# The gate stage of a decoder trunk: squares written three tiles behind their tanh, and tanh results in four tiles of their own

## The chip, the core and the metric

The kernel runs on one core of a Trainium2 chip, as one launch. The metric is the device time of that launch in microseconds. Three executions of the kernel before took 2317.64, 2319.58 and 2322.39 us; the median, 2319.58 us, is the time that the change is measured against. The core has engines that run side by side and wait for each other by semaphores: PE (TensorE, the matmuls), DVE (VectorE), ACT (ScalarE), POOL (GpSimd) and SP (SyncE, which here only issues DMAs). Each engine works its own list of instructions strictly in the order in which it was built.

## The reference

Two layers work on an activation x of 512 tokens by 1024 features, all in float32. Per layer:

```
h  = RMSNorm(x)
A, B = attention(h), time mixing(h)        (two token mixers)
x += RMSNorm((sigmoid(gA)*A + sigmoid(gB)*B) @ W_out)
x += RMSNorm(W_down(gelu(a)*b)),  [a,b] = conv3(RMSNorm(x) @ W_up)
x += RMSNorm(sigmoid(x @ W_pg) * (p[i] @ W_ple))      <- the gate stage
```

The last line is the stage that the change touches. RMSNorm divides by the root of the mean square over the 1024 features of a token, so its factor for a token is known only once all eight feature tiles have been squared and summed.

## The kernel before, in words

x lies transposed: eight tiles (KT = 8) of 128 features by 512 tokens. The tokens are worked in two halves of 256 (`HALVES`, line 29), so that one half's norm can run beside the other half's matmuls. Weights and activations are split into a high and a low part, and each product is three matmuls, high by high, high weight by low activation, low weight by high activation (`mm3`, lines 250 to 252). In the trace the split parts have the names wh and wl or kwh and kwl (weights), xh and xl (x as the gate stage reads it), hh and hl (the next layer's input). A high part is written by ACT, a low part by DVE.

**The gate stage** is `pg`, a call of the generator `lin` (lines 945 to 979) that is resumed by `next(pg)` once for each half (line 1049). Per half it makes eight output tiles. The first three are interleaved over the eight feature tiles of x (`deep` = 3), so that they can start as soon as the first tile of x is final; the other five follow one after another. Each tile has 24 matmuls of 128x256. The results go to PSUM: tiles 0 to 2 of both halves and tiles 3 to 7 of the first half use the buffers pm, pm and pf (`PM`, line 102); tiles 3 to 7 of the second half use the pool of three buffers `PS`, under the name half (line 111).

When a tile is complete, `done` (line 950) does four things for it: ACT takes the tanh out of PSUM into a tile tg (line 1029), which frees the PSUM buffer; DVE makes yo = (tg + 1) * yo (line 1030); ACT squares yo into sq (`addsq`, line 293; the first tile's square goes straight to acc); and DVE adds sq to acc. tg and sq come from one pool S of four buffers. When all eight have been added, `rstd` (lines 279 to 291) makes the norm factor: PE sums acc over the partitions (ssq, line 284), DVE makes nv, a seed nry and three Newton steps (each nrt, nrt, nry), and PE spreads the factor over the partitions (rstd, line 290). `post_norm` (line 334) then makes, per feature tile, yo = yo * g * rstd and x = x + yo, on DVE.

The same `rstd` and `post_norm` stand ahead of the gate stage, for the result of W_down. There they hand over each x tile to `scaled`, which writes xh and xl for the gate matmuls. The second half of that norm runs beside the gate stage's first half.

**After the gate stage** of layer 0 come `seam` and `lead` (lines 1077 and 217): post_norm of each half, with hh and hl, and the first matmuls of the next layer (lead, and pm<-hh). After that of layer 1 comes the end of the kernel: post_norm of the first half, then of the second, and the DMAs of x.

**What sets the order.** The lists of the engines are made at build time by a scheduler with priorities. The order in which the Python code emits instructions is an instruction's priority; `turn` (line 1062) raises it for the norms, and for the second half holds the norm back behind a named matmul (`pin`). So the place at which `done` emits an instruction decides where it comes to stand in an engine's list, and also what the scheduler puts ahead of it.

Of the kernel before, what the change touches and what calls it, by code (L numbers as in the profile page):

```python
# [55 lines left out]
class Trunk:  # L56
# [287 lines left out]
    @staticmethod  # L344
    def row(t, k):
        return t[k * P:(k + 1) * P, :]
# [491 lines left out]
    def run(self):  # L838
        nc, tc, a = self.nc, self.tc, self.a
# [9 lines left out]
        G = self.alloc(xpool, "N", 30)  # L849
        A, S = self.alloc(xpool, "A", 4), self.alloc(xpool, "S", 5)  # L850
# [11 lines left out]
        for l in range(self.L):  # L862
# [68 lines left out]
            for m in range(KT):  # L931
                ps = self.proj(a["w_or"][l, m], yact)
# [9 lines left out]
            fp = xstack.enter_context(tc.tile_pool(name=f"ff{l}", bufs=1))  # L942
            G, X, Y, A, S = (self.alloc(fp, n, b) for n, b in (("G", 44), ("X", 8), ("Y", 8), ("A", 3), ("S", 4)))

            def lin(src, act, ys, ws, evac, n, deep=1, extra=None):

                acc = A("acc")
                self.res = ys, acc

                def done(m, ps, hs):  # L950
                    self.addsq(acc, evac(ys[m][:, hs], ps[:, hs], m, hs), hs, m == 0, S)
                for m in range(n):
                    if deep == 2 and m == 1:
                        raws = [self.raw_w(src(i), P, G) for i in range(n, KT)]
                    if deep == 2 and m == 2:
                        ws = [self.split_raw(r, G) for r in raws]
                    done(m, self.proj(src(m), act), slice(0, T))
                    if extra and 0 < m <= 4:
                        extra(m - 1)
                yield  # L960
                ws = [self.load_wk(src(n), S)] if ws is None else ws
                for hs in HALVES:
                    one = hs is HALVES[0]
                    pss = [self.PM("x") if i < 3 else self.PS("half") for i in range(deep)]
                    for k in range(len(act)):
                        for i in range(deep):
                            x_ = self.mm3(pss[i][:, hs], ws[i][k], tuple(x[:, hs] for x in act[k]), k == 0, k == len(act) - 1)
                        if k == 5:
                            self.pin = x_
                    for i in range(len(ws)):  # L970
                        if i < deep:
                            ps = pss[i]
                        else:
                            ps = self.PM("x") if i < 3 or one else self.PS("half")
                            self.proj_half(ps, ws[i], act, hs)
                        done(n + i, ps, hs)
                    if one:
                        yield
                yield
# [4 lines left out]
            ed = self.dt(f"ed{l}")  # L984
            ys = [Y("yo") for _ in range(KT)]
            wo = lin(lambda m: a["w_out"][l, m], mixed, ys, None, copy, 4, 2)
            next(wo)
            xs = []
# [18 lines left out]
            for m in range(KT):  # L1007
# [3 lines left out]
                ps = self.PM("f") if m % 2 else self.PT("ple")  # L1011
                for k, w in enumerate(self.whole(a["w_ple"][l, m], P, self.cls)):
# [6 lines left out]
            ys = [Y("yo") for _ in range(KT)]  # L1019
            gw = []  # L1020
            dn = lin(lambda m: a["w_dn"][l, m], u, ys, None, copy, KT - 1,
                     extra=lambda m: gw.append(self.keep_w(a["w_pg"][l, m], P, H)))
            next(dn)
# [1 line left out]
            fin = self.res  # L1025

            def ple(y, ps, m, hs):
                tg = S("tg")
                self.act(tg[:, hs], ps, AF.Tanh, scale=0.5)
                self.stt(y, tg[:, hs], 1.0, y, ALU.add, ALU.mult)  # L1030
                return y
            xa = [(G("xh", F32R), G("xl", F32R)) for _ in range(KT)]
            ys = []
            graw = [self.raw_w(a["w_pg"][l, m], P, G) for m in range(6, KT)]
            pg = lin(lambda m: a["w_pg"][l, m], xa, ys, gw, ple, 0, 3)
            next(pg)
            for hs in HALVES:
                with self.turn(hs):
                    self.post_norm(*fin, vv("fpost"), NORM_EPS, xs, hs, lambda k: self.scaled(xs[k], None, xa[k], hs))
                if hs is HALVES[0]:  # L1040
                    next(dn)
                    if hs is HALVES[0]:
                        with self.behind():
                            gw += [self.whole(a["w_pg"][l, m], P, "mf"[m - 4]) for m in range(4, 6)]
                            gw += [self.split_raw(r, G) for r in graw]
                            ys += [G("yo") for _ in range(KT)]
                            for m in range(KT):
                                self.dma(ys[m], row(ed, m))
                next(pg)
            ys, acc = self.res  # L1050
# [151 lines left out]
```

## Time and profile before

| | |
|---|---|
| median of three executions | 2319.58 us |
| profiled execution | 2329.03 us |
| its span, first to last instruction | 2327.3 us |
| mean granted TensorE clock over the span | 0.981 |
| PE busy | 2228.8 us, 96% of the span |
| DVE, ACT, POOL busy | 66%, 48%, 1% |
| gate stage of layer 0, matmuls | about 1116 to 1172 us |
| gate stage of layer 1, matmuls | about 2263 to 2308 us |

A row of the timeline reads: start, duration, engine, line, operation, output<-inputs, shape, count, and in brackets how long the engine had been idle and what ended that. Matmuls are pipelined, so that two of 0.28 us may start 0.12 us apart. "PEclk" in a table of windows is the TensorE clock that was granted, 1.00 being full speed. Lines are those of the kernel before; 125, 128 and 134 are the helpers `act`, `tt` and `stt`, so that a group there is known by its tile.

### The profile page before, as it was taken

What the parts mean: (1) busy time and instruction counts of PE and PEld (TensorE: products, weight loads), DVE (VectorE), ACT (ScalarE), POOL (GpSimd) and SP (SyncE); (2) the same over time, 40 slices, a digit from 0 to 9 for tenths busy, and PEclk for the clock granted to TensorE, in tenths of its full rate; (3) what the DMA queues carried; (4) which work ended last, traced back from release to release, by engine and by line L of the source; (5) the groups of instructions that cost most, each with busy time, mean ns of one, the idle gap of its engine ahead of it and who ended that gap; (6) DMA issues with size and microseconds to landing.
All of it is one profiled execution on the core that took longest, in us unless ns stands there. A gap on an engine that the chain in (4) does not pass through costs nothing. (4 is left out here: it accounts for less than half of the span.)

```text
span 2327.3 us, 39473 instructions
## 1 busy us (share of the span) xinstructions
PE 2228.8 (96%) x14340; PEld 1740.2 (75%) x14340; DVE 1546.9 (66%) x3683; ACT 1109.6 (48%) x2450; POOL 27.1 (1%) x86
## 2 busy tenths in 40 slices
PE   7999999999999999999899999998999999999997
PEld 6766776667689777788896677766777887777886
DVE  6764678767566777743877647778656667776346
ACT  5566455544444544432445655545443544444332
POOL 1000000000000000000000000000000000000000
PEclk9999999889999999999999999999999999999998
DMA  4532332245571423233234333333356623223432
GB/s 150 168 94 97 99 94 79 75 121 171 176 259 31 128 91 98 89 118 116 86 124 148 98 104 98 83 92 103 113 159 212 213 78 92 95 95 90 126 98 69
DMA packets 204515, 269.40 MB, mean 116 GB/s; under 512 B 71840, under 2 KB 84640, under 8 KB 204320
## 3 DMA queue, kind: packets, MB, share of 16 engines
q1 hardware_dynamic: 204320, 266.88, 37.3%
q8 instruction: 113, 1.85, 0.3%
q14 instruction: 82, 0.67, 0.1%
HBM read 218.95 MB, written 42.47 MB: 112 GB/s over the span
## 5 line engine op out<-in xcount | busy, mean ns | idle before, releaser
L155 DVE TENSOR_TENSOR wl<-w,wh 128x512 fp32r<-128x512 f32 (+2 forms) x574 | 373.9, 662 | 317.4 <-ACT wh L125 292.7
L125 ACT ACTIVATE wh<-w 128x512 fp32r<-128x512 f32 (+1 forms) x590 | 348.8, 604 | 477.8 <-PE pm L251 134.7
L250 PE MATMUL pm<-hh,wh 128*128 128x512 f32 x1040 | 423.0, 412 | 4.6 <-ACT wh L125 2.4
L252 PE MATMUL pm<-hh,wl 128*128 128x512 f32 x1040 | 417.1, 408 | 7.4 <-DVE wl L155 7.2
L251 PE MATMUL pm<-hl,wh 128*128 128x512 f32 x1040 | 416.3, 404 | 0.0
L250 PEld LDWEIGHTS pm<-hh,wh 128*128 128x128 f32 x1040 | 196.8, 189 | 63.3 <-ACT wh L125 11.2
L252 PEld LDWEIGHTS pm<-hh,wl 128*128 128x128 f32 x1040 | 196.9, 189 | 57.5 <-DVE wl L155 13.6
L251 PEld LDWEIGHTS pm<-hl,wh 128*128 128x128 f32 x1040 | 197.4, 190 | 44.1 <-issue 7.2
L250 PE MATMUL pf<-hh,wh 128*128 128x512 f32 x512 | 208.3, 407 | 9.5 <-ACT hh L125 3.6
L251 PE MATMUL pf<-hl,wh 128*128 128x512 f32 x512 | 203.7, 398 | 0.0
L252 PE MATMUL pf<-hh,wl 128*128 128x512 f32 x512 | 203.5, 398 | 0.1
L134 DVE SCALAR_TENSOR_TENSOR cv<-un,vec,cv 128x511 f32<-128x511 f32 (+1 forms) x176 | 130.5, 749 | 40.6 <-ACT cv L125 38.1
L250 PEld LDWEIGHTS pf<-hh,wh 128*128 128x128 f32 x512 | 96.2, 188 | 42.7 <-ACT wh L125 8.5
L252 PEld LDWEIGHTS pf<-hh,wl 128*128 128x128 f32 x512 | 96.6, 189 | 27.0 <-issue 4.4
L251 PEld LDWEIGHTS pf<-hl,wh 128*128 128x128 f32 x512 | 96.7, 189 | 19.6 <-issue 1.8
L125 ACT ACTIVATE cv<-un,vec 128x512 f32<-128x512 f32 x88 | 71.1, 814 | 66.7 <-DVE un L128 66.7
L250 PE MATMUL pm<-uh,wh 128*128 128x512 f32 (+1 forms) x248 | 89.2, 360 | 3.5 <-ACT wh L125 3.4
L252 PE MATMUL pm<-uh,wl 128*128 128x512 f32 (+1 forms) x248 | 89.3, 360 | 0.0
L251 PE MATMUL pm<-ul,wh 128*128 128x512 f32 (+1 forms) x248 | 88.9, 359 | 0.0
L128 DVE TENSOR_TENSOR acc<-acc,sq 128x256 f32<-128x256 f32 (+1 forms) x114 | 50.0, 463 | 31.2 <-ACT sq L125 30.5
L533 DVE CUSTOM_DVE_ANT_0 sm<-scores,tmask 128x256 f32<-128x256 f32 (+1 forms) x128 | 43.5, 385 | 37.3 <-PE scores L117 37.1
L697 DVE TENSOR_TENSOR Z<-rin,Z 128x126 f32<-128x126 f32 (+22 forms) x248 | 62.3, 251 | 4.3
(409 smaller groups left out, 4468.9 us busy)
## 6 DMA issues: line engine op xcount, KB each, us to landing
w<-in_w_up_dram SPq DMA_DIRECT2D x156, 256.0 KB
w<-in_w_dn_dram SPq DMA_DIRECT2D x80, 256.0 KB
w<-in_w_q_dram SPq DMA_DIRECT2D x32, 256.0 KB
w<-in_w_ga_dram SPq DMA_DIRECT2D x32, 256.0 KB
w<-in_w_k_dram SPq DMA_DIRECT2D x32, 256.0 KB
w<-in_w_r_dram SPq DMA_DIRECT2D x32, 256.0 KB
w<-in_w_v_dram SPq DMA_DIRECT2D x32, 256.0 KB
w<-in_w_gb_dram SPq DMA_DIRECT2D x32, 256.0 KB
```

The source lines that it names most:

```text
L125: return self.nc.scalar.activation(out=out, in_=in_, func=func, **kw)
L128: return self.nc.vector.tensor_tensor(out=out, in0=in0, in1=in1, op=op)
L134: return self.nc.vector.scalar_tensor_tensor(out=out, in0=in0, scalar=s, in1=in1, op0=op0, op1=op1)
L155: self.nc.vector.tensor_tensor(out=wl, in0=w, in1=wh.bitcast(F32), op=ALU.subtract)
L250: mm(ps, wh, ah, start=start, stop=False)
L251: mm(ps, wh, al, start=False, stop=False)
L252: return mm(ps, wl, ah, start=False, stop=stop).ins
L533: nc.vector.tensor_tensor_reduce(out=sm[i][:, par * 256:par * 256 + KW], in0=scs[par][:, x * 256:x * 256 + KW], in1=tm, scale=1.0, scalar= ...
L697: nc.vector.tensor_tensor(out=tv, in0=rin[:, jj:jj + 1, jj + 1:].broadcast_to([P, n, nt]), in1=zt[:, :n, jj:jj + 1].broadcast_to([P, n, nt ...
```

## The change

`lin` has a new parameter, `lag`. `done` still emits the tanh and the yo at once, but puts the square on a list, and emits it only when more than `lag` squares wait; at the end of a half the list is emptied. The gate stage asks for a lag of 3, all other calls for 0, which is the order of before. And tg no longer comes from the pool S, which it shared with sq, but from four tiles of the pool G (44 buffers), taken in turn.

```
-            def lin(src, act, ys, ws, evac, n, deep=1, extra=None):
+            def lin(src, act, ys, ws, evac, n, deep=1, extra=None, lag=0):
 
                 acc = A("acc")
                 self.res = ys, acc
 
+                late = []
+
                 def done(m, ps, hs):
-                    self.addsq(acc, evac(ys[m][:, hs], ps[:, hs], m, hs), hs, m == 0, S)
+                    late.append((evac(ys[m][:, hs], ps[:, hs], m, hs), hs, m == 0))
+                    flush(lag)
+
+                def flush(n):
+                    while len(late) > n:
+                        self.addsq(acc, *late.pop(0), S)
...
                         done(n + i, ps, hs)
+                    flush(0)
                     if one:
                         yield
...
             def ple(y, ps, m, hs):
-                tg = S("tg")
+                tg = tgs[m % 4]
...
-            pg = lin(lambda m: a["w_pg"][l, m], xa, ys, gw, ple, 0, 3)
+            pg = lin(lambda m: a["w_pg"][l, m], xa, ys, gw, ple, 0, 3, lag=3)
...
                             ys += [G("yo") for _ in range(KT)]
+                            tgs = [G("tg") for _ in range(4)]
```

No arithmetic is added or removed. What changes is the lists. Three places matter.

On ACT, in layer 0, where the second half of the gate stage meets the post_norm of the first half (hh is the next layer's input; tg<-half is the tanh of tiles 3 to 7). Before:

```order
L125 ACTIVATE tg<-pf 128x256
L125 ACTIVATE wh<-w 128x512 x2
L125 ACTIVATE hh<-x,vec 128x256 x4
L125 ACTIVATE acc<-yo 128x256
L125 ACTIVATE sq<-yo 128x256
L125 ACTIVATE tg<-pm 128x256
L125 ACTIVATE sq<-yo 128x256
L125 ACTIVATE tg<-half 128x256
```

and now:

```order
L125 ACTIVATE tg<-pf 128x256
L125 ACTIVATE tg<-pm 128x256
L125 ACTIVATE hh<-x,vec 128x256 x2
L125 ACTIVATE tg<-half 128x256
L125 ACTIVATE wh<-w 128x512
L125 ACTIVATE hh<-x,vec 128x256
L125 ACTIVATE acc<-yo 128x256
L125 ACTIVATE tg<-half 128x256
```

The first tanh out of a half buffer stood behind four hh, the acc and two squares, each of which waits for DVE; it now stands behind two hh.

On PE, in layer 0, right after the three interleaved tiles of the first half (rstd is that of the second half of the W_down norm). The difference:

```order
 L251 MATMUL pm<-xl,kwh 128x256
 L252 MATMUL pm<-xh,kwl 128x256
+L290 MATMUL rstd<-ident,nry 128x128 x2
+L250 MATMUL half<-xh,kwh 128x256
+L250 MATMUL half<-xh,wh 128x256 x2
+L251 MATMUL half<-xl,kwh 128x256
+L252 MATMUL half<-xh,kwl 128x256
+L250 MATMUL half<-xh,kwh 128x256
```

In all 15 matmuls into half follow the rstd there; the first half's tiles 3 (pf, 24 matmuls) and 4 (pm, 24) come behind them. Before, tile 3 and two matmuls of tile 4 stood ahead of rstd, the other 22 of tile 4 behind it, and then 64 matmuls into half. 49 of these 64 now stand at the end of the second half's interleaved tiles, 57 matmuls into half in a row there; and 12 matmuls pm<-hh of the next layer, which stood at that place, come after the whole gate stage. The same happens in layer 1 with 9 matmuls instead of 15.

On PE, at the very end of layer 1 (the ssq and rstd of the last norm, first half and second half):

```order
 L251 MATMUL half<-xl,kwh 128x256
 L252 MATMUL half<-xh,kwl 128x256
+L284 MATMUL ssq<-ones_83,acc 128x1 x2
 L290 MATMUL rstd<-ident,nry 128x128 x2
 L284 MATMUL ssq<-ones_83,acc 128x1 x2
 L290 MATMUL rstd<-ident,nry 128x128 x2
```

The added row is the first half's ssq, which stood 48 matmuls earlier, ahead of the tiles 6 and 7 of the second half, and now follows them. On DVE the Newton steps of the first half move with it, behind the last tile.

## The prediction

> **What bounds the kernel now.** I began with the page's busy row, then asked for the tanh tile's waits, and then read PE's timeline around both gate stages.
>
> ```profile
> PE 2228.8 (96%) x14340; PEld 1740.2 (75%) x14340; DVE 1546.9 (66%) x3683; ACT 1109.6 (48%) x2450; POOL 27.1 (1%) x86
>   ACT sq L125: 11.6, 21
>   PE half L250: 5.0, 1
> ```
>
> PE sets the time: it is busy for 96% of the span, so an edit on ACT is worth what it does to PE's list. The last two rows are from the view of the tile tg, of those who waited for it: squares waited 11.6 us, on ACT, which is off the path; PE waited once, 5.0 us. That wait is the only thing in 2327 us that the lag can remove directly. Here it stands, PE first, then ACT, then the windows with busy time of each engine and PEclk:
>
> ```profile
> 1163.57 0.58 PE L250 MATMUL half<-xh,kwh 128*128 128x256 f32 x1 [5.00 <-ACT tg L125]
> ...
> 1169.50 0.41 PE L250 MATMUL half<-xh,kwh 128*128 128x256 f32 x1
> 1169.87 0.28 PE L252 MATMUL half<-xh,kwl 128*128 128x256 f32 x1
> 1169.99 0.28 PE L250 MATMUL half<-xh,kwh 128*128 128x256 f32 x1
> 1163.15 0.37 ACT L125 ACTIVATE tg<-half 128x256 f32<-128x256 f32 x1
> 1163.50:1166.00 2.50, 2.43 (x11) 2.43 (x12) 1.74 (x6) 1.56 (x6) 0.00 (x0) 0.50 0.32 106
> ```
>
> PE needs a fourth half buffer of three; the first comes free with the tanh at 1163.15, which stood behind hh and squares. After the idle 5.00 us the clock is at 0.50 (last column but two) until 1169.7: matmuls start every 0.213 us (1163.57 to 1169.50: 28 matmuls), then every 0.12 us (1169.87 to 1169.99). 29 slow ones lose 29 * (0.213 - 0.12) = 2.7 us. So layer 0 can gain 5.0 + 2.7 = **7.7 us**. In layer 1 the timeline of PE shows no idle time at all from the interleaved tiles to the last matmul into half; there nothing is to be gained.
>
> **The change part by part.** The tanh, squares and adds stay what they were; their own tiles cost nothing, since G has room and no DMA or copy is added. The costs lie in PE's new list.
>
> *The removed wait.* In the new list 57 matmuls into half (57 * 0.12 = 6.8 us) stand between the interleaved tiles and the first matmul that needs a freed buffer, and the tanh that frees it stands behind two hh instead of four hh, acc and squares. What hides the tanh is those matmuls; without them the 5 us would be back. I count the full gain, **-7.7 us**. The bound on the other side is that the tanh still waits for some hh: at most the 5 us.
>
> *The early rstd, layer 0.* Now rstd follows the interleaved tiles at once. PE of before:
>
> ```profile
> 1121.76 0.36 PE L250 MATMUL pf<-xh,kwh 128*128 128x256 f32 x1
> 1126.18 0.68 PE L290 MATMUL rstd<-ident,nry 128*128 128x128 f32 x4 [1.07 <-DVE nry L134]
> 1129.33 0.28 PE L250 MATMUL half<-xh,kwh 128*128 128x256 f32 x1
> ```
>
> and DVE and ACT, which make the factor and then xh:
>
> ```profile
> 1119.70 0.16 DVE L131 TENSOR_SCALAR nv<-ssq 128x2 f32<-128x2 f32 x1 [0.48 <-PE ssq L284]
> 1121.73 0.15 DVE L134 SCALAR_TENSOR_TENSOR nrt<-nrt,nv 128x2 f32<-128x2 f32 x1
> 1122.24 0.69 DVE L128 TENSOR_TENSOR kwl<-raw,kwh 128x512 fp32r<-128x512 f32 x1 [0.35 <-ACT kwh L125]
> 1125.28 0.69 DVE L155 TENSOR_TENSOR wl<-w,wh 128x512 fp32r<-128x512 f32 x1 [0.80 <-ACT wh L125]
> 1125.88 0.15 DVE L134 SCALAR_TENSOR_TENSOR nry<-nrt,nry 128x2 f32<-128x2 f32 x1
> 1126.90 0.87 DVE L134 SCALAR_TENSOR_TENSOR yo<-yo,vec,rstd 128x256 f32<-128x256 f32 x2 [0.53 <-PE rstd L290]
> 1124.61 0.63 ACT L125 ACTIVATE wh<-w 128x512 fp32r<-128x512 f32 x1 [1.61 <-DMA w<-in_w_pg_dram]
> 1128.14 0.76 ACT L125 ACTIVATE xh<-x 128x256 fp32r<-128x256 f32 x2 [1.32 <-DVE x L128]
> 1129.88 0.42 ACT L125 ACTIVATE xh<-x 128x256 fp32r<-128x256 f32 x1 [0.98 <-DVE x L128]
> ```
>
> Before, PE did tile 3 in this time and waited only 1.07 us. Now it has nothing from 1121.76 on. In the new list of DVE the wl of 1125.28 stands behind the last nry, and the tanh that held back kwh is gone. The remaining steps are two kwl (0.61 each, from 1121.8) and, among them, seven small steps of 0.19 after the nrt of 1121.73: last nry at 1124.1, and with the 0.30 from 1125.88 to 1126.18, rstd at 1124.4. The gain for the norm is thus 1.8 us, but DVE does the wl next, which still ends at 1125.88 (its wh comes from a DMA at 1124.61), so that the first yo starts at 1125.9 instead of 1126.90, and all xh come 1.0 us sooner: the third at 1128.88 to 1129.3. The 15 half matmuls need the first three xh; and tile 3 waits for a buffer whose tanh stands behind the third xh on ACT (0.37 us more). Tile 3 so begins at 1129.7. At that time before had issued tiles 3 and 4, 48 matmuls by 1129.33, and 3 more by 1129.7. After has issued 15. PE is behind by (51 - 15) * 0.12 = **+4.3 us**. The other end: if xh came a further 0.8 us sooner (wl not in the way), +3.5.
>
> *The clock.* That stretch holds two idle times, 1121.9 to 1124.4 (2.5 us) and 1125.1 to about 1127.5 (2.4 us), with one rstd between. What does such a gap do? Two places of this trace, the row after the gap and a window behind it:
>
> ```profile
> 87.46 0.55 PE L250 MATMUL pf<-hh,wh 128*128 128x512 f32 x1 [2.37 <-ACT hh L125]
> 93.00:95.00 2.00, 2.00 (x7) 1.58 (x6) 1.45 (x3) 1.32 (x3) 0.00 (x0) 0.60 0.65 204
> 628.78 0.50 PE L250 MATMUL pm<-yr,wh 128*128 128x512 f32 x1 [2.17 <-ACT yr L125]
> 629.00:632.00 3.00, 3.00 (x13) 2.00 (x12) 1.13 (x2) 0.41 (x1) 0.00 (x0) 1.00 0.82 285
> ```
>
> 2.37 us of idle time cost the clock. A mean of 0.60 over the two microseconds from 93 is 1.6 us at 0.5 and 0.4 at 1.0, so that it came back at 94.6, 7.1 us after the restart. 2.17 us cost nothing. Ours lie just above the first and come twice, so I take the drop. It ends about 6 us after the steady work starts at 1129.7, or 7 us after the rstd of 1124.4, when only 2 us of work would be slow: between 0.9 and 2.7 us; I take **+2.4 us**, near the 2.7 that the restart at 1163.57 cost, since here too steady work starts cold. The end below is no drop, 0.
>
> [...]
>
> *Layer 0 in sum:* -7.7 + 4.3 + 2.4 = -1.0 us (-3.4 without the drop).
>
> *The early rstd, layer 1.* The same, without the gain:
>
> ```profile
> 2268.78 0.36 PE L250 MATMUL pf<-xh,kwh 128*128 128x256 f32 x1
> 2271.83 0.68 PE L290 MATMUL rstd<-ident,nry 128*128 128x128 f32 x4
> 2272.47 0.28 PE L250 MATMUL pm<-xh,wh 128*128 128x256 f32 x1
> 2274.40 0.76 DVE L128 TENSOR_TENSOR xl<-x,xh 128x256 fp32r<-128x256 f32 x2
> ```
>
> Here the wl stands inside the Newton steps in both lists, and only the missing tanh and a shorter wait for kwh help: rstd at 2271.4 instead of 2271.83, 0.43 sooner, with 2.5 us of idle time ahead of it and some 1.7 behind. The low part of the second x tile, the last that the nine half matmuls need, is done at 2275.15 - 0.43 = 2274.7, and tile 3 starts at 2274.8. Before had issued 24 + 21 by then (pm from 2272.47, a matmul every 0.12). Behind by (45 - 9) * 0.12 = **+4.3 us**, and with the clock as in layer 0 **+2.4 us** (from 0 to 2.7).
>
> *The moved ssq, layer 1.* The last rows of PE and DVE:
>
> ```profile
> 2301.37 0.50 PE L284 MATMUL ssq<-ones,acc 128*128 128x1 f32 x4
> 2301.97 0.39 PE L250 MATMUL half<-xh,kwh 128*128 128x256 f32 x1
> 2307.70 0.28 PE L252 MATMUL half<-xh,kwl 128*128 128x256 f32 x1
> 2307.82 0.60 PE L290 MATMUL rstd<-ident,nry 128*128 128x128 f32 x4
> 2317.25 1.19 PE L290 MATMUL rstd<-ident,nry 128*128 128x128 f32 x4 [6.49 <-DVE nry L134]
> 2308.83 0.87 DVE L134 SCALAR_TENSOR_TENSOR yo<-yo,gple,rstd 128x256 f32<-128x256 f32 x2
> 2309.62 0.42 DVE L128 TENSOR_TENSOR acc<-acc,sq 128x256 f32<-128x256 f32 x1
> 2314.99 0.15 DVE L131 TENSOR_SCALAR nv<-ssq 128x2 f32<-128x2 f32 x1
> 2316.94 0.16 DVE L134 SCALAR_TENSOR_TENSOR nry<-nrt,nry 128x2 f32<-128x2 f32 x1
> ```
>
> Before, the first half's ssq and Newton steps lay inside tiles 6 and 7; its post_norm began at 2308.83, 1.0 us after the last matmul into half (next slot 2307.82), and DVE is busy from there to the end but for the second rstd's wait. Now ssq takes that slot, nv follows some 0.55 later (DVE's idle 0.48 for ssq before the nv of 1119.70, and the start), nv to the last nry takes 2316.94 - 2314.99 = 1.95, the tile's own yo and acc in between 0.42 each (the acc of 2309.62), nry to the first yo 1.0 (1125.88 to 1126.90 above). That is 0.55 + 1.95 + 0.84 + 1.0 = 4.3 us after the slot instead of 1.0: +3.3. That acc no longer stands inside the post_norm, -0.4, and the ssq no longer takes 0.5 us out of the matmuls (2301.37 to 2301.97, less one slot of 0.12). **+2.4 us** (ends 1.6 and 3.3, by whether yo and acc fit into the pauses of the small steps and whether the acc was ever in the way). What follows, eight yo and x, the second half's steps and its post_norm, has the same order as before, and moves as one block.
>
> *Layer 1 in sum:* 4.3 + 2.4 + 2.4 = +9.1 us.
>
> *Both:* -1.0 + 9.1 = **+8.1 us**. The durations are those of the profiled execution, 2329.03 us, whose span is 2327.3; it lies 0.4% above the median, and even if all its rows are too long by as much, 0.4% of 8 us is nothing. So 2319.58 + 8.1 = 2327.7; I forecast **2327.5 us**.
>
> One price is not in this sum. The lead's weights in layer 0 are split later: on ACT two wh that stood ahead of the hh now stand among the late squares, and the lead needs them right after the last matmul into half, on a PE that is 1 us earlier than before.
>
> **The rivals.** Within 0.2% of before, 4.6 us, a measurement of this kernel, whose three runs spread over 4.75 us, tells no change from one.
>
> 1. *The forecast:* both early rstd leave PE idle, the clock drops in both layers, and the tail moves. 0.53, 2327.5; its own range is 2324.5 to 2330.
>
> 2. *The idle times stand, the clock holds.* For it: 2.5 us is barely more than 2.37, and 2.17 held. Against it: there are two pauses in a row. Price: 8.1 - 2 * 2.4 = +3.3, 2322.9 us, within 0.2%. If it drops in one layer only, 2325.3. 0.22 for the clock holding in both. [...]
>
> 3. *The lead waits too.* In layer 0 the next layer's lead finds its weights, or its own rstd, late. For it: the lists, as just said. Against it: DVE and ACT are busy for 66% and 48% and have room. Two splits and their low parts, at the wh of 1124.61 and the wl of 1125.28, are 2 * (0.63 + 0.69) = +2.6, so 2330.3; with a clock drop behind that wait 2332.7. 0.12.
>
> 4. *Faster.* The norm's factor is there when PE arrives. Then the 15 and 9 early matmuls do not wait, layer 0 keeps its 7.7 us, and layer 1 pays the tail alone: -7.7 + 2.4 = -5.3, 2314.3 us. The deciding point is the last nry of the early norm: it would have to come at 1121.5 instead of 1124.1, and the xh by 1122. For it: without the tanh, ACT and DVE reach kwh and kwl sooner than I reckon. Against it: from nv at 1119.70 five low parts of 0.6 us, like the kwl of 1122.24, and nine small steps do not fit into 1.8 us, whatever ACT does. 0.08.
>
> 5. *The change does nothing that PE sees:* the lag frees the half buffers no sooner, and the early rstd only trades one idle time for another: 2319.6 to 2321. 0.05.
>
> **How the numbers follow.** Slower by over 0.2% (above 2324.2): cases 1 and 3, 0.65, with the single drop of case 2 counted in 1. Within 0.2%: cases 2 and 5, 0.27. Faster: case 4, 0.08. The predicted time is that of case 1. The range reaches down to 2318, which takes in case 2 (2322.9 with the spread of a median, some 2 us) and most of 5, and up to 2332.7 for case 3; what is left out is case 4 and the far ends.
>
> **What would show it.** In the profile after, layer 0: no PE row of half with 5 us idle time near 1160; an rstd with about 2.5 us of idle time before it, right behind the interleaved tiles, and a first half<-xh,kwh with about 2.4 more; PEclk near 0.5 in the 4 to 6 us behind. Layer 1: the same pair at about 2271, but no gain later; the ssq of the first half after the last matmul into half, and about 4 us from it to the first yo<-yo,gple. The interleaved tiles of layer 1 should stand about 1 us earlier than before, and the end about 8 later. The prediction is wrong in its sign if the early rstd finds its nry done; it is wrong in size if PEclk stays at 1.00 behind the two rstd, or if tiles 3 to 5 of either half wait for a tg tile, of which there are four.

## The result, and the profile after

The changed kernel took 2337.84 us (median of 7 executions, 2328.49 to 2349.37), the kernel before in the executions beside it 2320.51 us (7, 2317.64 to 2325.36; the three known ones are among them). The ratio is 1.0072, with a 95% interval from 1.0049 to 1.0096: slower by 17 us, where +8 was forecast, and outside the range of 2318.0 to 2332.7. The profiled execution of the change has a span of 2336.5 us.

Read the same places as in the prediction. First the timeline of PE in layer 0, then the windows (busy time of the engines, PEclk in the last column but two):

```profile
1115.95 0.28 PE L252 MATMUL pm<-xh,kwl 128*128 128x256 f32 x1
1118.67 0.68 PE L290 MATMUL rstd<-ident,nry 128*128 128x128 f32 x4 [2.44 <-DVE nry L134]
1121.67 0.58 PE L250 MATMUL half<-xh,kwh 128*128 128x256 f32 x1 [2.32 <-ACT xh L125]
...
1125.04 0.41 PE L250 MATMUL pf<-xh,kwh 128*128 128x256 f32 x1
...
1126.45 0.28 PE L251 MATMUL pf<-xl,kwh 128*128 128x256 f32 x1
```

```profile
1116.00:1118.00 2.00, 0.23 (x2) 0.03 (x1) 1.90 (x9) 0.00 (x0) 0.00 (x0) 1.00 0.83 217
1120.00:1122.00 2.00, 0.33 (x1) 0.33 (x2) 2.00 (x7) 0.75 (x2) 0.00 (x0) 0.50 1.03 384
1124.00:1126.00 2.00, 2.00 (x11) 2.00 (x11) 2.00 (x7) 0.92 (x3) 0.00 (x0) 0.50 0.02 7
1164.00:1170.00 6.00, 5.96 (x51) 5.65 (x49) 1.22 (x3) 2.97 (x8) 0.00 (x0) 1.00 0.19 60
```

The rstd stands right behind the interleaved tiles and waits 2.44 us, the first half matmul another 2.32 us, and the clock is at 0.50 until 1126.3. In return the stage's end, 1164 to 1170, is full of work at clock 1.00; the 5.0 us wait is gone.

The same in layer 1 (the wait before rstd is 2.71 us here, and 2.45 us in every other profile with the early rstd), and then the end of the kernel (PE, DVE):

```profile
2268.47 0.28 PE L252 MATMUL pm<-xh,kwl 128*128 128x256 f32 x1
2271.46 0.68 PE L290 MATMUL rstd<-ident,nry 128*128 128x128 f32 x4 [2.71 <-DVE nry L134]
2273.89 0.58 PE L250 MATMUL half<-xh,kwh 128*128 128x256 f32 x1 [1.75 <-ACT xh L125]
2274.00:2280.00 6.00, 6.00 (x28) 6.00 (x29) 5.09 (x15) 2.16 (x7) 0.00 (x0) 0.50 0.04 13
2314.12 0.50 PE L284 MATMUL ssq<-ones,acc 128*128 128x1 f32 x4
2317.33 0.98 PE L290 MATMUL rstd<-ident,nry 128*128 128x128 f32 x4 [2.71 <-DVE nry L134]
2318.35 0.87 DVE L134 SCALAR_TENSOR_TENSOR yo<-yo,gple,rstd 128x256 f32<-128x256 f32 x2 [1.16 <-PE rstd L290]
```

From these rows the two stages can be measured alone. I take as stage 0 the time from the first pf<-xh of layer 0 to the rstd<-ident,rcol of layer 1 (the first point behind seam and lead that all lists share), as stage 1 the time from the first pf<-xh of layer 1 to the end of the span, and as the rest what lies outside both. All eleven profiled executions of this study:

```
profile of                       stage 0   stage 1   the rest   span
before                            91.65     67.77    2167.9    2327.3
before, copied                    90.51     67.80    2168.8    2327.1
change                            90.68     77.15    2168.7    2336.5
change, again                     90.95     76.87    2157.1    2324.9
change, third                     91.82     76.62    2160.2    2328.6
tiles alone                       91.73     75.93    2158.2    2325.9
change in layer 0 alone           92.78     67.78    2165.1    2325.7
change in layer 1 alone           90.54     76.59    2167.7    2334.8
lag alone                         85.18     70.87    2168.0    2324.0
lag in layer 0, shared pool       84.58     67.80    2165.6    2318.0
lag in layer 0, shared, again     84.54     67.74    2161.2    2313.5
```

Where the code of a stage is that of before, it takes 90.5 to 91.7 and 67.7 to 67.8 us. With the change (four profiles for each stage) it takes 90.7 to 92.8 and 76.6 to 77.2. By the means the stages cost (91.6 - 90.9) + (76.8 - 67.8) = 0.7 + 9.0 = **9.7 us**; the 0.7 is no more than the single values scatter. And the rest, whose work is the same but for a few rows of layer 1's lists, varies over 12 us from one execution to the next. It holds between 15 (change, again) and 22 (change) stretches of 3.41 us at half clock, of which the last section tells more; each costs about 1.7 us (half of 3.41), so that the seven of difference are worth 12 us. That is where the difference between 10 and 17 us has to be looked for.

### The profile page after: what moved, and what is told of

The parts are those of the page before. It is cut to its first block, busy times and chain, and to the rows that moved or that the text cites. A ratio compares the mean times of both kernels' runs of the same rounds, so it can differ in the third digit from the quotient of the medians.

```text
span 2336.5 us, 39461 instructions
## 1 busy us (share of the span) xinstructions
PE 2234.1 (96%) x14340; PEld 1746.0 (75%) x14340; DVE 1547.7 (66%) x3683; ACT 1110.6 (48%) x2450; POOL 26.8 (1%) x86
## 5 line engine op out<-in xcount | busy, mean ns | idle before, releaser
L250 PEld LDWEIGHTS pm<-hh,wh 128*128 128x128 f32 x1040 | 196.9, 189 | 62.8 <-ACT wh L125 10.3
L251 PEld LDWEIGHTS pf<-hl,wh 128*128 128x128 f32 x512 | 97.2, 190 | 19.6 <-issue 1.8
```

What stands on the lines that cost most here:

```text
L250: mm(ps, wh, ah, start=start, stop=False)
L251: mm(ps, wh, al, start=False, stop=False)
```

## The experiments

Timed executions of the kernel before stood beside each set; 89 of them in all have a mean of 2324.2 us (2312 to 2342, standard deviation 6.3). Since single executions scatter so much, I also give differences of means, with 95% intervals from the scatter of the single executions.

### Which part of the edit moves the lists

The lag alone, with the tanh results in the shared pool as before:

```
-                tg = tgs[m % 4]
+                tg = S("tg")
...
-                            tgs = [G("tg") for _ in range(4)]
```

> The lag of 3 stays, but the tanh results come from the pool S again, which they share with the squares. Theory 1 (the early rstd comes with the tanh tiles of their own, not with the lag): in both layers rstd stands where it stood before, tile 3 runs ahead of it, and PE's idle time before it is about 1 us, not 2.4; the end of layer 1 is as before; the 5.0 us wait and its 2.7 us of slow clock in layer 0 are gone, so 2320.5 - 7.7 = 2313 us (2311 to 2316). Theory 2 (the lag moves the rstd and the ssq): early rstd in both layers, 2328 to 2338 us as in the changed kernel.

and the four tiles alone:

```
-            pg = lin(..., ple, 0, 3, lag=3)
+            pg = lin(..., ple, 0, 3)
```

> The tanh results have four tiles of their own, the lag is 0. Theory 1 (the tiles make the whole change, the lag next to nothing beside them): early rstd in both layers with 2.4 us of idle time ahead of it and 2.3 (layer 0) and 1.7 (layer 1) behind, no 5 us wait, the ssq of the first half after the last matmul; the time of the changed kernel, 2328 to 2340 us. Theory 2 (the lag does it): the time of before, 2318 to 2325 us, with the 5 us wait.

Measured: the lag alone 2324.12 us, ratio 0.9990 (0.9965 to 1.0016); the tiles alone 2337.06 us, ratio 1.0041 (1.0014 to 1.0067), in means +9.9 +- 4.3; both against 35 executions of before with median 2327.25. PE of the tiles alone, and of the lag alone:

```profile
1111.11 1.19 PE L290 MATMUL rstd<-ident,nry 128*128 128x128 f32 x4 [2.44 <-DVE nry L134]
1114.29 0.58 PE L250 MATMUL half<-xh,kwh 128*128 128x256 f32 x1 [1.98 <-ACT xh L125]
2261.83 1.19 PE L290 MATMUL rstd<-ident,nry 128*128 128x128 f32 x4 [2.45 <-DVE nry L134]
2264.78 0.58 PE L250 MATMUL half<-xh,kwh 128*128 128x256 f32 x1 [1.75 <-ACT xh L125]
```

```profile
1121.78 0.68 PE L290 MATMUL rstd<-ident,nry 128*128 128x128 f32 x4 [1.16 <-DVE nry L134]
2265.43 0.68 PE L290 MATMUL rstd<-ident,nry 128*128 128x128 f32 x4
2300.62 0.50 PE L284 MATMUL ssq<-ones,acc 128*128 128x1 f32 x4
2304.97 0.88 PE L290 MATMUL rstd<-ident,nry 128*128 128x128 f32 x4 [3.84 <-DVE nry L134]
```

Theory 1 holds: what costs is the tiles. With them, and no lag, the rstd comes early in both layers with the same waits as in the changed kernel; with the lag and no tiles it stands where it stood, and the wait before it is 1.16 us (layer 1: none). That is the opposite of how the two halves of the edit look in the diff. The 5.0 us wait is gone with either half, with the tiles through the matmuls that the new list puts in its place. The lag alone does what it was made for: stage 0 is 85.18 us, and there is no slow clock in it. But its time was forecast 7.7 us under that of before, and its mean is 2.6 +- 4.3 under; stage 1 is 3.1 us longer than before, which I had missed. The squares of the first half's last tiles now come late, ssq follows the tiles 6 and 7, and PE waits 3.84 us for the Newton steps at the very end. So the late ssq, unlike the early rstd, comes with either half: in layer 1 the tiles alone cost 8.2 us, the lag alone 3.1, and both together 9.0. Why the tiles bring the rstd forward in the list, when the scheduler builds it, is not settled.

### Layer 0 or layer 1

The whole change for one layer, the code of before for the other (`lag=3 if l == 0 else 0`, tg from `tgs` or from S by the layer):

> The whole change in layer 0, the code of before in layer 1. By the two profiles the gate stage of layer 0 gains 1.3 us up to the attention of layer 1. Theory 3 (the further 9 us of the median, beyond the two gate stages, are clock drops in layer 1's attention and time mixing that the earlier start of that layer brings about): 2320.5 - 1.3 + 9 = 2328 us, with more slow clock between 1230 and 1660 us than the kernel before. Theory 4 (they are the luck of which runs were taken): 2319 us (2317 to 2322).

> The code of before in layer 0, the whole change in layer 1. By the two profiles the last 59 us become 9.4 us longer, of which about 3.4 are slow clock. Both theories of the median's further 9 us say the same here, since everything ahead of this gate stage is as before: 2320.5 + 9.4 = 2330 us (2327 to 2333). More than 2334 us would speak for a third cause, a cost of this stage that the profile of the changed kernel doesn't show.

Measured: layer 0 alone 2322.56 us, ratio 0.9991 (0.9967 to 1.0016); layer 1 alone 2334.05 us, ratio 1.0032 (1.0008 to 1.0057). As means: -2.5 +- 3.9 and +7.9 +- 4.4 us. Theory 3 falls: the change in layer 0, with its shift of all that follows, costs nothing that can be measured, where 7.7 us more than before were expected. The difference sits in layer 1's stage, +8.8 us in its profile. As plain times both came out just above what was expected (2322 for theory 4, and the 2334 that was to speak for a third cause), but these were reckoned from 2320.5 us, and the kernel before stood at 2327.25 in this set; against it, layer 0 alone agrees with the -1.3 of theory 4 and layer 1 alone with the forecast +9.4.

### How far executions of one program lie apart

> The kernel before, with one empty line added at the end of the file. It tells how far two sets of executions of one program lie apart. Theory A (single executions differ by several us through clock drops that come and go): this median within 4 us of that of the kernel before, single times over a range of 15 to 30 us, and the slower an execution, the lower its mean clock, about 0.9 us for each us of lost clock. If the executions lay within 5 us as the three first ones did, theory A would be wrong.

> The changed kernel once more, beside more runs of the kernel before. Theory A (the two gate stages make the whole difference; the rest of the first comparison's 17 us is the luck of which executions were slowed by clock drops elsewhere): the stage of layer 0 takes within 1.5 us of before, that of layer 1 is 9 us longer, and the mean is 7 to 11 us over the mean of the kernel before, 2334 to 2337 us if that is 2326 again. Theory B (the change brings on clock drops elsewhere): 14 us or more over the kernel before.

> The changed kernel a third time. Its two stages have been 9 us longer in both profiles; the mean over its first fourteen executions was about 14 us above the kernel before, beside which they ran. If the stages make the whole difference, 7 to 11 us over the mean of the kernel before; if the change also meets more slow clock elsewhere, 12 us or more.

Measured: the copy of before 2327.66 us (12 executions, 2314.32 to 2333.37), against 2320.12 for the kernel before in the same set (24); ratio 1.0022 with an interval of 1.0003 to 1.0041, for the same instructions. The two medians lie 7.5 us apart, where theory A allowed 4; the range of 19 us is as it said. Medians of the four sets of before: 2320.5, 2327.3, 2320.1, 2325.5. The change again: 2330.05 (7 executions), ratio 1.0050 (1.0028 to 1.0071), in means +11.3 +- 4.3; a third time: 2333.89 (12), ratio 1.0044 (1.0022 to 1.0066), +10.4 +- 4.5. The first comparison was +16.8 +- 5.0 in means. Over all executions whose clock is on record a regression of the time on the mean granted clock gives 0.85 us for each us of lost clock, and with it the scatter falls from over 6 us to 2.3. At an equal clock the copy lies 0.2 +- 1.6 us from the kernel before, and the three sets with clocks within 1.3 us of each other: what sets them apart is slow clock too. The intervals here know the scatter of single executions only, and may be too narrow.

So theory A stands, in its 7 to 11 us by the two later comparisons together: +10.9 +- 3.1 us, which holds the stages' 9.7. The profiles show no sign of theory B either: in the rest the three of the change have 22, 15 and 16 slow stretches of 3.41 us, the other eight 17 to 22. The first comparison had a kernel before whose seven executions lay 3 us under its long mean of 2324, and seven of the change that lay 2 over its mean of 2335.5 (26 executions). All three together are +12.5 +- 2.6; whether a further 1 to 3 us beside the stages are real, these runs don't settle.

### A version that keeps the gain

The lag in layer 0 alone, tanh results from the shared pool (against the kernel before; `lin` has its `lag` as in the change):

```
-            pg = lin(..., ple, 0, 3)
+            pg = lin(..., ple, 0, 3, lag=3 if l == 0 else 0)
```

> Lag of 3 in layer 0 alone, tanh results from the shared pool S as before, layer 1 as before. The run with the lag alone had its layer 0 stage 6.5 us shorter and its last stage 3.1 us longer, the latter because the squares of the first half come late at the very end. Theory: 6 to 7 us under the kernel before (2320 if that is 2326), no 5 us wait in layer 0, the last stage at 67.8 us as before. Rival (the lag only trades the wait for another one further on): within 3 us of the kernel before.

> The lag in layer 0 alone with the shared pool, again. Its layer 0 stage was 6 to 7 us shorter than before in the profile and nothing else differed. If that is the whole difference, the mean is 4 to 8 us under that of the kernel before; within 2 us of it would say that the gain is lost elsewhere.

Measured: 2316.15 us, ratio 0.9993 (0.9974 to 1.0012), and 2321.47 us, ratio 0.9984 (0.9964 to 1.0004); in means -1.7 +- 4.5 and -4.9 +- 4.2. In both profiles stage 0 is 84.6 us, 6.3 less than before, and stage 1 is that of before. The rows that replace the 5.0 us wait:

```profile
1125.07 0.68 PE L290 MATMUL rstd<-ident,nry 128*128 128x128 f32 x4 [1.02 <-DVE nry L134]
1162.42 0.30 PE L250 MATMUL lead<-hh,kwh 128*32 128x256 f32 x1 [0.51 <-ACT tg L125]
1158.00:1164.00 6.00, 5.50 (x47) 5.26 (x46) 3.17 (x7) 3.80 (x10) 0.00 (x0) 1.00 0.37 119
```

The stage shows the gain plainly, against the rival. The whole time does not clear its scatter in either comparison, only in both together, and barely (-3.4 +- 3.1 us); in means the first alone came out within the rival's 3 us, the second within the 4 to 8 us of the theory. At an equal clock, by the regression, which takes out what the two slow stretches behind the wait cost, it is -4.5 and -4.2, each +- 1.7 or less.

## Why the prediction was right and wrong

**The sum was nearly right.** +8.1 us stood against 9.7 in the stages and 10.9 +- 3.1 in the later executions; by layers, -1.0 against +0.7 and +9.1 against +9.0. Term by term:

- *The removed wait, -7.7 forecast.* The version with the lag in layer 0 has neither the wait nor the early rstd, and its stage is 84.56 against 90.9: **-6.3**. A wait of 0.51 us has taken the wait's place, at the lead, and one of 0.42 us stands at the stage's end mark, rstd<-ident,rcol.
- *The early rstd and its clock in layer 0, 4.3 + 2.4 = +6.7.* The change's stage 0 less that of this version: 91.6 - 84.6 = **+7.0**, of which the last point below explains some 0.6. The two idle times were 2.44 and 2.32 us, forecast 2.5 and 2.4. The split was a little off: tile 3 began 9.1 us after the last interleaved matmul (1115.95 to 1125.04), where 8.1 were reckoned (1121.64 to 1129.7), since at clock 0.50 the 15 half matmuls themselves became the limit (the tanh that frees tile 3's buffer was done at 1123.62); less slow work came behind. That "their own tiles cost nothing" was wrong as an attribution: the early rstd that this term prices comes with the tiles.
- *Layer 1, 4.3 + 2.4 + 2.4 = +9.1.* Measured **+9.0**, close to the parts forecast: up to the start of the last matmul into half 54.2 us instead of 48.2 (+6.0, forecast 6.7), behind it 22.7 instead of 19.6 (+3.1, forecast 2.4). The end: slot of the ssq to first yo 4.23 us (2314.12 to 2318.35), forecast 4.3.
- *The lead that waits, rival 3, at 0.12 and +2.6.* It comes and goes. In the third profile of the change, as in that of layer 0 alone (1.42 us), a row of the next layer's first matmuls, which wait for their split weights, shows it:

```profile
1166.00 0.91 PE L250 MATMUL pm<-hh,kwh 128*128 128x256 f32 x2 [1.11 <-ACT kwh L125]
```

  In the first two profiles of the change it is absent, and their stage 0 is 0.9 to 2.1 us shorter than in these two.

**The step that failed** is "So 2319.58 + 8.1": the base. Three executions between 2317.64 and 2322.39 were taken for the level of the kernel, and the profiled one, 9.45 us above, was set aside with the remark that 0.4% of 8 us is nothing. The level is 2324.2 us, with 6.3 of scatter, and the four medians of before differ by 7. The range was built from the bounds of the change's own terms, with some 2 us for the spread of a median at its lower end alone; nor was 0.2% what a few executions can tell apart. With 2324 the same sum gives 2332.3, and the range would have had to be some 6 us wider on each side.

The measured time lies 10.3 us above the forecast. Of these the base makes 4.6 us and the stages 1.8 (9.7 against 7.9). The luck of which executions were taken makes 2.3, by which the seven executions of the change lay above the long mean of 2335.5. The other 1.6 are what the long means differ by beyond the stages, and stay open. In the first comparison luck widened the difference from the other side too: the seven of before had a median 3.7 us under their level.

The trace of before could have warned of it. The prediction used its slow windows to price a gap, but didn't ask why this execution was 9 us above the others. One stretch may answer most of that; it is 23.9 us long in the profile of before and 3.4 us in that of the change, at the same place and with the same work:

```profile
398.36:422.28 23.92, 23.52 (x228) 16.53 (x227) 6.67 (x15) 5.38 (x15) 0.00 (x0) 0.50 0.25 58
```

```profile
399.28:402.68 3.40, 3.35 (x19) 2.48 (x19) 2.75 (x6) 0.63 (x1) 0.00 (x0) 0.50 0.27 42
```

These 20.5 us more at half clock are worth some 10 us. In the eleven profiles the stretch lasts from nothing to seven times 3.41 us, and up to 395 us all kernels have the same instructions in the same order on every engine. No profile of a fast execution of the kernel before was kept, so it isn't shown that the three first executions had a short one.

**Of the rivals**, the clock that holds (2) did not happen: the stages of both layers lost two low windows (6.8 us at 0.50) in every profile that has the early rstd. In the change two gaps of 2.44 and 2.32 us, and of 2.71 and 1.75 us, dropped the clock, with one rstd between. The drop was forecast because the gaps lie just above 2.37 us and come twice. By the counts in the last section the length of a gap alone does not decide, so the first reason was right by luck; the second is the one that carries. The faster case (4) did not happen: the last nry was late by what was reckoned.

**What the prediction gave as signs** came as written: the rows of layer 0 and 1, the ssq behind the last matmul, the 4 us behind it. One sign failed, that layer 1's interleaved tiles stand 1 us earlier than before: they began at 2259.35 and 2259.53. That time contains the rest, with its 12 us of scatter, and was no test.

## What to carry to other kernels

Cut the trace into the stages that a change touches and compare these, start to end, over two or more profiles; a total may scatter by more than the effect, and here the stages repeat within 1 to 2 us while the total moves by 20. When the profiled execution is not as fast as the timed ones, find out where before using either as the base. And take a two-part edit apart: its harmless-looking half (new tiles for an operand) moved PE's list and cost 9 us in the two stages, while the half with the idea in it was worth 6 us in the layer where PE had waited.

## What the runs showed of the hardware

In the traces of this study the low clock comes in whole windows. I worked out from the granted clock (PEclk) in windows of 2 us where each stretch at 0.50 begins and ends; two of the profiles (before, change; the stretch in which each execution ends, from 2313.3 and from 2317.6 on, is left out):

```
before: 87.8-94.6  398.4-422.3  480.3-483.7  494.0-507.6  1163.0-1169.8  1262.0-1265.4  1552.1-1555.5  1610.1-1613.5  1644.2-1654.5
in 3.413 us:  2.0   7.0   1.0   4.0   2.0   1.0   1.0   1.0   3.0
change: 88.7-95.5  399.3-402.7  471.0-477.8  488.0-501.7  1058.0-1061.5  1119.5-1126.3  1235.6-1242.4  1256.0-1262.8  1549.6-1553.0  1607.6-1611.0  1634.9-1655.4  2273.2-2280.0
in 3.413 us:  2.0   1.0   2.0   4.0   1.0   2.0   2.0   2.0   1.0   1.0   6.0   2.0
```

The period is read from these lists: the single stretches last 3.4 us, the one of seven 23.9, and the first begin and the last lie 1556.4 us apart in before and 2184.5 in the change, 456 and 640 periods of 3.413. Every stretch is a whole number of 3.413 us, and within one profile all begin at the same phase of that period to within 0.07 us (2.42 to 2.49 in before, 3.33 to 3.36 in the change), over 2200 us. The phase differs from profile to profile, of one program too: it is 3.34, 1.48 and 1.07 us in the three profiles of the change. So the low windows lie on a raster that the program doesn't set, and whether a pause costs the clock depends, by my estimate from the counts below, on how it lies to that raster. Each low window costs about 1.7 us of full-speed time (half of 3.41). That is most of the scatter of the totals (over 6 us, of which 2.3 are left at an equal clock): at 1235 the change lost two windows behind a pause of 0.94 us, where before lost none at the same work behind one of 1.23 us (before, then change):

```profile
1240.38 0.50 PE L250 MATMUL pf<-hh,wh 128*128 128x512 f32 x1 [1.23 <-ACT hh L125]
```

```profile
1233.40 0.49 PE L250 MATMUL pf<-hh,wh 128*128 128x512 f32 x1 [0.94 <-ACT hh L125]
1236.49 0.80 PE L252 MATMUL pm<-sgh,wl 128*128 128x512 f32 x1 [0.31 <-DVE wl L155]
```

What the traces show to matter is how much of one such window PE is busy. Here are the windows that hold the pause of 2.37 us ahead of 87.46 in before, the one of 2.17 us ahead of 628.78, which fell on two, and the wait for the early rstd in the change (the first number behind the comma is PE's busy time):

```profile
84.34:87.76 3.42, 1.05 (x5) 0.47 (x3) 3.06 (x5) 0.63 (x1) 0.00 (x0) 1.00 0.86 275
623.69:627.10 3.41, 2.92 (x13) 1.98 (x11) 2.44 (x4) 1.79 (x3) 0.00 (x0) 1.00 0.73 236
627.10:630.51 3.41, 1.73 (x7) 1.28 (x8) 1.43 (x3) 1.26 (x2) 0.00 (x0) 1.00 0.92 338
```

```profile
1116.08:1119.49 3.41, 0.83 (x6) 0.52 (x4) 2.40 (x12) 0.63 (x1) 0.00 (x0) 1.00 0.93 286
```

The first and the last, with PE busy for 31% and 24%, were followed by low windows; the two between, with 86% and 51%, were not. Counted over all eleven profiles, without their first and last 20 us: of the windows at full clock with PE busy below 45%, all 66 were followed by a low one, of those between 45% and 62%, 15 of 73 (the windows that hold the two pauses above lie there, with 62% in the change and 61% in before), and of those above, 30 of 6984. Each of these 30 holds two dozen or more matmuls of 32x32. Two pauses like those around the early rstd leave, at any phase, one window below 45%: in layer 1 at least 4.2 us of 4.9 are idle, so that of two windows one has 2.1 us idle or more, and PE is busy for 39% of it at most. That fits the drop in five of five profiles in each layer. This is a count and not a mechanism. The traces do not explain why the clock stayed low for one window at 399 in one profile and for seven in another, with PE busy for 23.5 of 23.9 us; no run here tells that.
